# Attention of a hybrid decoder trunk: the value table's two parts side by side, denominators summed on GpSimd, value products two key blocks behind the scores

## The chip, the cores and the metric

One core of one Trainium2 chip runs the whole program. The metric is the device time of one execution in microseconds. All times below are of the kernel before the change.

## The reference

Two decoder layers over 1024 tokens of 1024 features in float32. Layer 0 mixes by attention with a forget gate (8 heads of 64) beside a causal pooling mixer; layer 1 is an RWKV-7 time mix; after each mixer stands a SwiGLU block. The change touches the attention alone:

```python
def one_block(args):
    i, q_i, c_i = args
    q_pos = i * Q_BLOCK + jnp.arange(Q_BLOCK)
    logits = (jnp.einsum('bhqd,bhkd->bhqk', q_i, k).astype(jnp.float32) * scale
              + c_i[..., :, None] - cum[..., None, :])
    causal = key_pos[None, :] <= q_pos[:, None]
    p = jax.nn.softmax(jnp.where(causal, logits, -1e30), axis=-1)
    return jnp.einsum('bhqk,bhkd->bhqd', p.astype(v.dtype), v)
```

## The kernel before, in words

Activations lie with features on the partitions and 512 tokens (one `half`) on the free axis. A product that has to be exact to float32 is split: `part` (L257; its operations are L259 and L260) makes a rounded high part on ScalarE and the rest, the low part, on VectorE. `mm3` (L156) then issues three matmuls per block: high by high (L163), high by low (L164), low by high (L165). Weights are loaded and split the same way in `load_part` (L150 load, L151 ScalarE, L152 VectorE).

The attention, `fox`, works on pairs of heads `p` (0 to 3) and on a head `a` (0, 1) of the pair. For one head:

- `assemble` (L474) copies keys and queries into 128-row tables: high parts in one half of the rows (`own`), low parts in the other (`oth`). The values are transposed into `VH[a][:, :, own]` (high, L492) and `VL[a][:, :, own]` (low, L493). The other 64 columns of `VH` are ones and those of `VL` zeros, set once at the start by GpSimd.
- `maxima` (L496) takes row maxima of the scores; its VectorE reduction is L512. It uses the same PSUM tiles `s` (two) as the scores.
- `attend` (L525) runs 12 steps: for the first half of the queries (`hq` 0) the key blocks `j` 0 to 3, for the second 0 to 7. A step's width `w` is 512 queries, or 384, 256, 128 on the diagonal. `scores` issues two or three matmuls into `s` (L538, L539, mask L541), then ScalarE's exponential `pt` (L543), its rounded part `ph` (a ScalarE cast, L121) and the rest `pl` on VectorE (L547). `values`, one step later, adds three matmuls into the PSUM tile `o`: `VH` by `ph` (L556), `VH` by `pl` (L557), `VL` by `ph` (L558). Because of the ones in `VH`, the other 64 rows of `o` hold the denominator. After the last block of a `hq` the logarithm, a sum with the gate, an exponential and a product (L563 to L566) write the result into `y`.

The order of work is set by `weave`: after each `yield c` of `attend`, the generators beside it are advanced by `c` times their weight. They are the next head's `assemble` and `maxima` (weight 0.5), and a filler of weight 2.8 to 3.2: for `a` = 0 the projections of the next pair (`prep`, with `head`, L425), for `a` = 1 up to three pooling units (`pool_group`, seven in all, L580 to L612, whose parts `pp` are made at L586 and L587 and multiplied at once) and an output gate; for the pair 3 the output projection. A scheduler then places each engine's instructions in one fixed order. Every engine works through its own queue in that order and waits at the head of it.

```python
        for st in steps:
            live.append(scores(*st))
            yield 2 * live[-1][4] / HN + 0.3
            if len(live) > 1:
                yield values(*live.pop(0))
```

GpSimd has few instructions in this part: the pooling unit's small copies and products (L592, L595, L608, L609). The PSUM tile `t` exists once; `head_mean` (L276 to L278), the transposes of `assemble` (L490) and of `maxima` (L518) take turns in it. Scratch tiles `tmp` rotate through five buffers.

Of the kernel before, what the change touches and what calls it, by code (L numbers as in the profile page):

```python
# [9 lines left out]
F32 = mybir.dt.float32  # L10
# [6 lines left out]
P = 128  # L17
# [296 lines left out]
def fox(k, ins, H, hpool, xpools, y, then, r_att):  # L314
# [65 lines left out]
    QB = [ap_.tile([P, S], F32R, tag=f"QB{a}", name=f"QB{a}") for a in range(2)]  # L380
    VH = [ap_.tile([P, 8, P], F32R, tag=f"VH{a}", name=f"VH{a}") for a in range(2)]
    VL = [ap_.tile([P, 8, P], F32R, tag=f"VL{a}", name=f"VL{a}") for a in range(2)]
    for a in range(2):
        own = slice(64 * a, 64 * a + 64)
        oth = slice(64 - 64 * a, 128 - 64 * a)
        nc.gpsimd.memset(QB[a][oth].bitcast(F32), 0.0)
        nc.gpsimd.memset(KB[a][oth].bitcast(F32), 0.0)
        nc.gpsimd.memset(KB[a][64 - 64 * a:72 - 64 * a].bitcast(F32), 1.0)
        nc.gpsimd.memset(VH[a][:, :, oth].bitcast(F32), 1.0)
        nc.gpsimd.memset(VL[a][:, :, oth].bitcast(F32), 0.0)  # L390

# [33 lines left out]
    def head(p, which, half, hl):  # L425

        g = gq if which == "q" else cvec(k, "k_gain")
        o = yield from project(hl, half)
        sq = tmp("asq")[:, 0:HN]
        nc.scalar.activation(sq, o, AF.Square)  # L430
        ms = head_mean(k, sq, [ap_.tile([P, HN], F32R, tag=t, name=nm(k, t), bufs=2) for t in ("ph", "pl")], (onesR, ep[half]))
        yield 3
        ars = tmp("ars")[:, 0:HN]
        nc.scalar.activation(ars, ms, AF.Ln)
        nc.scalar.activation(ars, ars, AF.Exp, scale=-0.5)
        t = ap_.tile([P, HN], F32, tag="a" + which, name=nm(k, "a" + which), bufs=2)
        nc.vector.scalar_tensor_tensor(t, o, g, ars, ALU.mult, ALU.mult)
        getattr(R[p], which)[half] = t
# [35 lines left out]
    def assemble(p, a):  # L474
# [18 lines left out]
        nc.vector.tensor_tensor(VL[a][:, :, own], pvb, rd(VH[a][:, :, own]), ALU.subtract)  # L493
# [31 lines left out]
    def attend(p, a):  # L525

        steps = [(a, hq, j) for hq in range(2) for j in range(4 * hq + 4)]
        live = []
        out = {}

        def scores(a, hq, j):
# [10 lines left out]
            pt = ap_.tile([P, HN], F32, tag="pt", name=nm(k, "pt"), bufs=2)  # L542
            nc.scalar.activation(pt[:, 0:w], s[:, 0:w], AF.Exp, bias=ncumT[:, j, h:h + 1])  # L543
            ph = ap_.tile([P, HN], F32R, tag="ph", name=nm(k, "ph"), bufs=2)
            pl = ap_.tile([P, HN], F32R, tag="pl", name=nm(k, "pl"), bufs=2)
            copy_to(k, CE[2], ph[:, 0:w], pt[:, 0:w])
            nc.vector.tensor_tensor(pl[:, 0:w], pt[:, 0:w], rd(ph[:, 0:w]), ALU.subtract)  # L547
            return a, hq, j, q0, w, ph, pl

        def values(a, hq, j, q0, w, ph, pl):  # L550
# [6 lines left out]
            nc.tensor.matmul(oo, VH[a][:, j], pl[:, 0:w], start=False, stop=False)  # L557
            nc.tensor.matmul(oo, VL[a][:, j], ph[:, 0:w], start=False, stop=(j == nj - 1))  # L558
            if j == nj - 1:
                own = slice(64 * a, 64 * a + 64)  # L560
                oth = slice(64 - 64 * a, 128 - 64 * a)
                den = tmp("den")[:, 0:HN]
                nc.scalar.activation(den[own], o[oth], AF.Ln)  # L563
                nc.vector.tensor_tensor(den[own], den[own], y[p][hq][own], ALU.add)
                nc.scalar.activation(den[own], den[own], AF.Exp, scale=-1.0)
                nc.vector.tensor_tensor(y[p][hq][own], o[own], den[own], ALU.mult)  # L566
            return 3 * w / HN

        for st in steps:
            live.append(scores(*st))  # L570
            yield 2 * live[-1][4] / HN + 0.3
            if len(live) > 1:
                yield values(*live.pop(0))
        for l in live:
            yield values(*l)

# [975 lines left out]
```

## Time and profile before

| what | value |
|---|---|
| time, median of 3 runs | 2701.54 us (2696.48 to 2703.55) |
| the profiled execution | 2699.03 us |
| its span in the trace | 2697.2 us |
| TensorE matmuls busy | 2633.8 us, 98% |
| VectorE busy | 1724.3 us, 64% |
| ScalarE busy | 1301.9 us, 48% |
| GpSimd busy | 50.6 us, 2% |
| attention, from 87 to 467 us: TensorE, VectorE, ScalarE busy | 374.30, 257.93, 213.77 of 380 us |

The profiled execution lies between the lowest and the median run. A matmul's row gives the time from its start to its modelled end; the next matmul starts before that end, so what a matmul takes from the queue is read from the start of one row to the start of the next. PE stands for TensorE's matmuls, PEld for its weight loads, DVE for VectorE, ACT for ScalarE, POOL for GpSimd. A wait row says which engine and line waited, and whose instruction ended the wait.

### The profile page before, as it was taken

The page shows a single profiled execution, that of the slowest core. Times are in us where ns is not written, and L with a number is a line of the kernel's source. Part 1 is how long each engine was busy: PE and PEld are TensorE (multiplying, and loading weights), DVE is VectorE, ACT ScalarE, POOL GpSimd, SP SyncE. Part 2 cuts the span into 40 slices and gives each one's busy share as a digit, 9 for nine tenths or more (in the row PEclk, how much of TensorE's full clock was granted, in tenths as well). Part 3 has the DMA queues.
Part 4 walks back from the last instruction along what each step waited for, and adds up shares of the span by engine and source line. Part 5 has one row for each costly group of instructions (what it writes and reads, how often), then busy time and mean ns, then how long its engine had stood idle before and what let it go on. Part 6 is the DMA issues. An engine that isn't in the chain of part 4 may idle for free.

```text
span 2697.2 us, 40269 instructions
## 1 busy us (share of the span) xinstructions
PE 2633.8 (98%) x15368; PEld 2080.5 (77%) x15368; DVE 1724.3 (64%) x2940; ACT 1301.9 (48%) x2299; POOL 50.6 (2%) x139
## 2 busy tenths in 40 slices
PE   8999999999999999999999999999999999999999
PEld 6787878788888777777777677777777778888887
DVE  8777684654446655975995685469768856634443
ACT  7555564442224765534634466664445444332232
POOL 1000000000001000000000000000000000000000
PEclk9999999999999999999999999999999999999999
DMA  4111131233333546424523534454344336333333
GB/s 136 58 52 55 44 98 48 83 97 96 96 98 114 168 162 191 129 82 123 160 87 100 194 101 161 160 182 128 91 141 134 93 100 199 109 98 94 98 98 94
DMA packets 170817, 307.03 MB, mean 114 GB/s; under 512 B 18928, under 2 KB 25968, under 8 KB 170624
## 3 DMA queue, kind: packets, MB, share of 16 engines
q1 hardware_dynamic: 156800, 279.29, 33.6%
q10 hardware_dynamic: 13824, 25.17, 2.5%
q8 instruction: 120, 1.97, 0.3%
q14 instruction: 73, 0.60, 0.1%
HBM read 257.96 MB, written 46.43 MB: 113 GB/s over the span
## 4 chain that ended last, share of the span: by engine, by line
PE 77%; DVE 14%; DMA 3%; ACT 3%; issue 2%; SPq 0%; DVEq 0%; ACTq 0%
PE mm L163 16%; PE mm L164 16%; PE mm L165 16%; PE fm L163 6%; PE fm L164 5%; PE fm L165 5%; DVE wlo L152 2%; PE mm L175 1%; DVE nu L1108 1%; DVE pd L1106 1%; DMA wraw<-in_wu_dram 1%; DVE ZL L1064 1%; ACT whi L151 1%; PE o L1173 1%; PE s L1161 1%
## 5 line engine op out<-in xcount | busy, mean ns | idle before, releaser
L151 ACT CAST whi<-wraw 128x512 fp32r<-128x512 f32 x738 | 453.7, 617 | 867.4 <-PE mm L164 478.7
L152 DVE TENSOR_TENSOR wlo<-wraw,whi 128x512 fp32r<-128x512 f32 x738 | 501.3, 684 | 449.6 <-ACT whi L151 441.1
L163 PE MATMUL mm<-hh,whi 128*128 128x512 f32 x864 | 344.1, 400 | 6.2 <-ACT hh L355 6.1
L165 PE MATMUL mm<-hh,wlo 128*128 128x512 f32 x864 | 338.4, 392 | 0.0
L164 PE MATMUL mm<-hl,whi 128*128 128x512 f32 x864 | 337.9, 392 | 0.0
L163 PE MATMUL mm<-uh,whi 128*128 128x512 f32 x728 | 283.6, 391 | 0.9 <-DVE x L1317 0.9
L165 PE MATMUL mm<-uh,wlo 128*128 128x512 f32 x728 | 283.1, 390 | 1.0 <-DVE wlo L152 1.0
L164 PE MATMUL mm<-ul,whi 128*128 128x512 f32 x728 | 283.2, 390 | 0.0
L163 PE MATMUL fm<-h1h,whi 128*128 128x512 f32 x528 | 220.2, 417 | 14.8 <-DVE sg L726 9.9
L164 PE MATMUL fm<-h1l,whi 128*128 128x512 f32 x528 | 210.3, 398 | 0.1
L165 PE MATMUL fm<-h1h,wlo 128*128 128x512 f32 x528 | 209.5, 397 | 0.5 <-DVE wlo L152 0.5
L163 PEld LDWEIGHTS mm<-hh,whi 128*128 128x128 f32 x864 | 162.3, 188 | 43.4 <-ACT hh L355 7.8
L165 PEld LDWEIGHTS mm<-hh,wlo 128*128 128x128 f32 x864 | 162.5, 188 | 34.4 <-issue 0.2
L164 PEld LDWEIGHTS mm<-hl,whi 128*128 128x128 f32 x864 | 162.7, 188 | 33.1 <-DVE hl L260 1.7
L163 PE MATMUL fm<-hh,whi 128*128 128x512 f32 x416 | 170.9, 411 | 3.3 <-ACT hh L259 2.3
L164 PE MATMUL fm<-hl,whi 128*128 128x512 f32 x416 | 164.9, 396 | 0.2 <-DVE hl L260 0.2
L165 PE MATMUL fm<-hh,wlo 128*128 128x512 f32 x416 | 164.6, 396 | 0.0
L163 PEld LDWEIGHTS mm<-uh,whi 128*128 128x128 f32 x728 | 136.5, 188 | 34.6 <-issue 3.5
L164 PEld LDWEIGHTS mm<-ul,whi 128*128 128x128 f32 x728 | 136.6, 188 | 30.9 <-issue 1.1
L165 PEld LDWEIGHTS mm<-uh,wlo 128*128 128x128 f32 x728 | 136.7, 188 | 30.1 <-DVE wlo L152 1.8
L705 DVE TENSOR_TENSOR x<-mm,x 128x512 f32<-128x512 f32 x96 | 66.3, 692 | 119.3 <-PE mm L165 119.2
L163 PEld LDWEIGHTS fm<-h1h,whi 128*128 128x128 f32 x528 | 100.6, 191 | 47.1 <-DVE sg L726 12.2
(338 smaller groups left out, 4645.4 us busy)
## 6 DMA issues: line engine op xcount, KB each, us to landing
wraw<-in_wg_dram SPq DMA_DIRECT2D x176, 256.0 KB, 2.8
wraw<-in_wu_dram SPq DMA_DIRECT2D x176, 256.0 KB, 2.7
wraw<-in_wd_dram SPq DMA_DIRECT2D x176, 256.0 KB, 2.7
wraw<-in_w_in_dram SPq DMA_DIRECT2D x52, 256.0 KB, 2.9
x<-in_xT_dram SPq DMA_DIRECT2D x32, 256.0 KB, 4.6
x<-x SPq DMA_DIRECT2D x32, 256.0 KB, 3.3
wraw<-in_w_k_dram SPq DMA_DIRECT2D x32, 256.0 KB, 2.8
wraw<-in_w_v_dram SPq DMA_DIRECT2D x32, 256.0 KB, 3.0
```

Of the source, the lines that this page charges most:

```text
L151: k.nc.scalar.copy(hi[0:p, 0:n], raw[0:p, 0:n])
L152: k.nc.vector.tensor_tensor(lo[0:p, 0:n], raw[0:p, 0:n], rd(hi[0:p, 0:n]), ALU.subtract)
L163: nc.tensor.matmul(out, wh, xh, start=(first and i == 0), stop=False)
L164: nc.tensor.matmul(out, wh, xl, start=False, stop=False)
L165: nc.tensor.matmul(out, wl, xh, start=False, stop=(last and i == n - 1))
L175: k.nc.tensor.matmul(out[n * q:n * q + n], w[:, n * j:n * j + n], xs[j], start=c == 0, stop=c + g == len(xs), tile_position=(0, n * q))
L705: nc.vector.tensor_tensor(X[half][m], o, X[half][m], ALU.add)
L1064: nc.vector.tensor_tensor(ZL[h][HS[1 - h], i, bs], s4[HS[1]], self.msk[HS[1]].rearrange("p a t -> p (a t)").unsqueeze(1).broadcast_to([64, ...
L1106: nc.vector.tensor_tensor(pv, nu[:, j + 1:32, j:j + 1].broadcast_to([P, n, j]), nu[:, j:j + 1, 0:j].broadcast_to([P, n, j]), ALU.mult)
L1108: nc.vector.tensor_tensor(nu[:, j + 1:32, 0:j], nu[:, j + 1:32, 0:j], pv, ALU.add)
L1161: nc.tensor.matmul(z[HS[h], i], ZL[h][:, i, c, 0:64], SV[h][:, i, c], start=True, stop=True)
L1173: nc.tensor.matmul(sp[HS[h], i], BK[h][:, i, c], uv[h][:, i], start=True, stop=True)
```

## The change

1. `VL` goes. The low part of the values is written into the columns of `VH` that held ones, so that one table has the high part in `own` and the low part in `oth`. A step's value products are two matmuls in place of three; `o` then holds high products in its `own` rows and low products in the others.
2. The denominators leave the matmuls. The exponentials of key block 0 go to a tile `da` (two buffers), and GpSimd adds each later block's `pt` to it. At the end of a `hq` the tile is split by `part` and summed over the partitions by two matmuls with `onesR` into `t`.
3. The end of a `hq` becomes a generator, `finish`. Its first half splits `da`, copies the low rows of `o` (ScalarE) and adds them to the high rows (VectorE). Its second half, one step later, holds the two matmuls and the former four operations. For `hq` 1 it runs after the last value product.
4. The value products run two steps behind the scores, and `ph` and `pl` have three buffers in place of two, in `head` too.

`part`, `tmp`, `pst` and `onesR` are those of before.

```diff
...
-        nc.gpsimd.memset(VH[a][:, :, oth].bitcast(F32), 1.0)
-        nc.gpsimd.memset(VL[a][:, :, oth].bitcast(F32), 0.0)
...
-        nc.vector.tensor_tensor(VL[a][:, :, own], pvb, rd(VH[a][:, :, own]), ALU.subtract)
+        nc.vector.tensor_tensor(VH[a][:, :, oth], pvb, rd(VH[a][:, :, own]), ALU.subtract)
...
-            pt = ap_.tile([P, HN], F32, tag="pt", name=nm(k, "pt"), bufs=2)
+            if j == 0:
+                pt = den[a, hq] = ap_.tile([P, HN], F32, tag="da", name=nm(k, "da"), bufs=2)
+            else:
+                pt = ap_.tile([P, HN], F32, tag="pt", name=nm(k, "pt"), bufs=2)
...
-            ph = ap_.tile([P, HN], F32R, tag="ph", name=nm(k, "ph"), bufs=2)
-            pl = ap_.tile([P, HN], F32R, tag="pl", name=nm(k, "pl"), bufs=2)
+            ph = ap_.tile([P, HN], F32R, tag="ph", name=nm(k, "ph"), bufs=3)
+            pl = ap_.tile([P, HN], F32R, tag="pl", name=nm(k, "pl"), bufs=3)
...
+            if j:
+                d = den[a, hq][:, q0 - hq * HN:]
+                nc.gpsimd.tensor_tensor(d, d, pt[:, 0:w], ALU.add)
...
-            nc.tensor.matmul(oo, VH[a][:, j], pl[:, 0:w], start=False, stop=False)
-            nc.tensor.matmul(oo, VL[a][:, j], ph[:, 0:w], start=False, stop=(j == nj - 1))
+            nc.tensor.matmul(oo, VH[a][:, j], pl[:, 0:w], start=False, stop=(j == nj - 1))
             if j == nj - 1:
-                own = slice(64 * a, 64 * a + 64)
-                oth = slice(64 - 64 * a, 128 - 64 * a)
-                den = tmp("den")[:, 0:HN]
-                nc.scalar.activation(den[own], o[oth], AF.Ln)
-                nc.vector.tensor_tensor(den[own], den[own], y[p][hq][own], ALU.add)
-                nc.scalar.activation(den[own], den[own], AF.Exp, scale=-1.0)
-                nc.vector.tensor_tensor(y[p][hq][own], o[own], den[own], ALU.mult)
+                ends.append(finish(a, hq, o, den[a, hq]))
             return 3 * w / HN
+
+        def finish(a, hq, o, d):
...
+            dh, dl = (ap_.tile([P, HN + 16], F32R, tag="tmp", name=nm(k, "dd"), bufs=k.tmpbufs)[:, 0:HN] for _ in range(2))
+            part(k, (dh, dl), d)
+            low = tmp("low")[:, 0:HN]
+            nc.scalar.copy(low[own], o[oth])
+            num = tmp("num")[:, 0:HN]
+            nc.vector.tensor_tensor(num[own], o[own], low[own], ALU.add)
+            yield 2
+            t = pst(k, "t", 1)
+            nc.tensor.matmul(t, onesR, dh, start=True, stop=False)
+            nc.tensor.matmul(t, onesR, dl, start=False, stop=True)
+            nc.scalar.activation(low[own], t[own], AF.Ln, scale=64.0)
+            nc.vector.tensor_tensor(low[own], low[own], y[p][hq][own], ALU.add)
+            nc.scalar.activation(low[own], low[own], AF.Exp, scale=-1.0)
+            nc.vector.tensor_tensor(y[p][hq][own], num[own], low[own], ALU.mult)
+            yield 0
 
         for st in steps:
             live.append(scores(*st))
             yield 2 * live[-1][4] / HN + 0.3
-            if len(live) > 1:
+            if ends and next(ends[0], None) is None:
+                ends.pop()
+            if len(live) > 2:
                 yield values(*live.pop(0))
         for l in live:
             yield values(*l)
+        for e in ends:
+            yield from e
```

Outside the attention the order of every engine is the same as before, but for GpSimd's settings at the start. Three places of the new order are looked at below.

TensorE at the end of head (0, 1), before the change (L538 to L541 scores, L556 to L558 values, L163 to L165 the filler):

```order
L538 MATMUL s_429_1795<-QA1_104,KA1_102 128x128
L539 MATMUL s_429_1795<-QB1_108,KB1_106 128x128
L541 MATMUL s_429_1795<-maskTR_94,identR_93 128x128
L556 MATMUL o_369_1560<-ph_427_1779,VH1_110 128x256
L557 MATMUL o_369_1560<-pl_428_1780,VH1_110 128x256
L558 MATMUL o_369_1560<-ph_427_1779,VL1_112 128x256
L538 MATMUL s_435_1820<-QA0_103,KA0_101 128x512
L539 MATMUL s_435_1820<-QB0_107,KB0_105 128x512
L541 MATMUL s_435_1820<-maskTR_94,identR_93 128x128
L163 MATMUL mm_445_1854<-hh_9_135,whi_439_1842 128x512
L164 MATMUL mm_445_1854<-hl_10_136,whi_439_1842 128x512
L556 MATMUL o_369_1560<-ph_431_1801,VH1_110 128x128
```

and with the change, from the last two value steps of that head on (L561 and L562 values, L579 and L580 the sum of `dd`, the split `da`, into `t`; L536 to L539 scores):

```order
L163 MATMUL mm_436_1776<-hh_100_386,whi_425_1721 128x512
L164 MATMUL mm_436_1776<-hl_101_387,whi_425_1721 128x512
L165 MATMUL mm_436_1776<-hh_100_386,wlo_426_1722 128x512
L561 MATMUL o_397_1623<-ph_439_1789,VH1_110 128x256
L562 MATMUL o_397_1623<-pl_440_1790,VH1_110 128x256
L561 MATMUL o_397_1623<-ph_443_1814,VH1_110 128x128
L562 MATMUL o_397_1623<-pl_444_1815,VH1_110 128x128
L579 MATMUL t_450_1843<-dd_446_1835,onesR_92 128x512
L536 MATMUL s_451_1850<-QA0_103,KA0_101 128x512
L537 MATMUL s_451_1850<-QB0_107,KB0_105 128x512
L539 MATMUL s_451_1850<-maskTR_94,identR_93 128x128
L580 MATMUL t_450_1843<-dd_447_1836,onesR_92 128x512
```

Before, the next head's scores and the filler follow the last values. Now the sum of the denominators stands right behind the last value product, its second half four rows on. Between the head's last mask matmul (six rows ahead of this piece) and L579 stand 12 matmuls.

TensorE in head (0, 0), with the change, where `head_mean` of the filler (L277, L278) and `finish` of `hq` 0 use the tile `t` one after the other:

```order
L165 MATMUL mm_270_1139<-hh_80_341,wlo_222_963 128x512
L163 MATMUL mm_270_1139<-hh_84_350,whi_221_962 128x512
L278 MATMUL t_267_1130<-pl_266_1127,bones_67 128x512
L164 MATMUL mm_270_1139<-hl_85_351,whi_221_962 128x512
L165 MATMUL mm_270_1139<-hh_84_350,wlo_222_963 128x512
L536 MATMUL s_273_1165<-QA0_103,KA0_101 128x512
L537 MATMUL s_273_1165<-QB0_107,KB0_105 128x512
L579 MATMUL t_271_1143<-dd_253_1084,onesR_92 128x512
L580 MATMUL t_271_1143<-dd_254_1085,onesR_92 128x512
```

Between the last matmul into one `t` and the first into the next stand four matmuls; before the change the next use of `t` behind this one came 30 matmuls later.

GpSimd in head (0, 1), with the change (L552 the additions to `da`, the other lines those of the pooling unit):

```order
L552 TENSOR_TENSOR da_315_1345<-da_315_1345,pt_339_1448 128x128
L614 COPY pu_349_1475<-halo_119 128x16
L552 TENSOR_TENSOR da_360_1504<-da_360_1504,pt_366_1535 128x512
L614 COPY pu_382_1584<-halo_119 128x16
L552 TENSOR_TENSOR da_360_1504<-da_360_1504,pt_377_1570 128x512
L617 COPY halo_119<-pu_382_1584 128x16
L630 TENSOR_TENSOR x_385_1592<-pb_384_1589,fc_221 128x16
L631 TENSOR_TENSOR x_385_1592<-x_385_1592,pu_382_1584 128x16
L552 TENSOR_TENSOR da_360_1504<-da_360_1504,pt_400_1642 128x512
```

Before, the rows L614 to L631 stood there alone; now the additions share the queue with them, and one addition stands behind a product that waits for VectorE's pooling sums.

## Rows read from the trace of the kernel before

**Rows 1.** The page: busy time of each engine; shares of the last chain.

```profile
PE 2633.8 (98%) x15368; PEld 2080.5 (77%) x15368; DVE 1724.3 (64%) x2940; ACT 1301.9 (48%) x2299; POOL 50.6 (2%) x139
...
PE 77%; DVE 14%; DMA 3%; ACT 3%; issue 2%; SPq 0%; DVEq 0%; ACTq 0%
```

**Rows 2.** Windows: stretch; busy PE, PEld, DVE, ACT, POOL; clock; DMA share, GB/s.

```profile
87.00:467.00 380.00, 374.30 (x1796) 304.28 (x1795) 257.93 (x531) 213.77 (x393) 7.92 (x24) 1.00 0.18 57
...
250.00:270.00 20.00, 19.36 (x87) 15.02 (x87) 19.56 (x44) 11.02 (x19) 2.08 (x5) 1.00 0.25 85
...
sum 80.00, PE 77.42 PEld 60.37 DVE 75.43 ACT 50.88 POOL 5.02; mean PE 19.35 PEld 15.09 DVE 18.86 ACT 12.72 POOL 1.26
...
sum 80.00, DVE 11.70; mean DVE 2.92
```

**Rows 3.** Timeline of TensorE, 461 to 465 us: start, duration, line, operation.

```profile
461.05 0.33 PE L558 MATMUL o<-ph,VL 128*128 128x384 f32 x1
461.22 0.39 PE L163 MATMUL mm<-hh,whi 128*128 128x512 f32 x1
461.45 0.40 PE L164 MATMUL mm<-hl,whi 128*128 128x512 f32 x1
...
463.88 0.28 PE L558 MATMUL o<-ph,VL 128*128 128x256 f32 x1
464.00 0.39 PE L163 MATMUL mm<-hh,whi 128*128 128x512 f32 x1
...
464.85 0.28 PE L558 MATMUL o<-ph,VL 128*128 128x128 f32 x1
464.97 0.44 PE L163 MATMUL mm<-hh,whi 128*128 128x512 f32 x1
```

**Rows 4.** Waits, 87 to 470 us: who <- for whom: total us, times, longest.

```profile
PEld o L557 <- DVE pl L547: 4.1, 11, 0.6
...
PEld o L556 <- ACT ph L121: 2.3, 4, 0.9
...
PE mm L163 <- ACT pp L586: 1.6, 5, 0.4
...
PE o L557 <- DVE pl L547: 1.2, 5, 0.4
...
PE o L556 <- ACT ph L121: 1.0, 2, 0.5
```

**Rows 5.** Groups by shape, 87 to 470 us: busy, mean ns; idle before, releaser.

```profile
L547 DVE TENSOR_TENSOR pl<-pt,ph 128x512 fp32r<-128x512 f32 x48 | 33.0, 687 | 12.4 <-ACT ph L121 11.9
...
L121 ACT CAST ph<-pt 128x512 fp32r<-128x512 f32 x48 | 29.7, 620 | 2.0 <-PE o L558 0.9
...
L564 DVE TENSOR_TENSOR den<-den,x 64x512 f32<-64x512 f32 x16 | 11.0, 686 | 7.8 <-ACT den L563 7.7
...
L434 ACT ACTIVATE ars<-t 128x512 f32<-128x512 f32 x12 | 7.2, 598 | 14.4 <-PE t L278 14.4
...
L543 ACT ACTIVATE pt<-s,ncumT 128x128 f32<-128x128 f32 x16 | 5.8, 362 | 5.2 <-PE s L541 5.2
```

**Rows 6.** GpSimd's groups by shape, whole span; same columns.

```profile
L389 POOL MEMSET VH<- 128x512 f32 x2 | 1.1, 527 | 0.1
```

**Rows 7.** Timelines of GpSimd and VectorE at 148, 250 and 865 us.

```profile
147.94 0.53 POOL L592 COPY pu<-halo 128x16 f32<-128x16 f32 x1 [27.82 <-DVE x L610]
...
147.73 0.89 DVE L152 TENSOR_TENSOR wlo<-wraw,whi 128x512 fp32r<-128x512 f32 x2
...
250.69 0.22 POOL L609 TENSOR_TENSOR x<-x,pu 128x16 f32<-128x16 f32 x1
...
250.22 0.69 DVE L512 CUSTOM_DVE_ANT_0 s<-s,bc 128x512 f32<-128x512 f32 x1
...
864.99 1.37 POOL L773 COPY x<-hlast 128x1 f32<-128x1 f32 x1
...
865.03 1.29 DVE L152 TENSOR_TENSOR wlo<-wraw,whi 128x512 fp32r<-128x512 f32 x2
```

More of the change, by code (lines that the diff above doesn't have):

```diff
@@ L381, in fox @@
     VH = [ap_.tile([P, 8, P], F32R, tag=f"VH{a}", name=f"VH{a}") for a in range(2)]
-    VL = [ap_.tile([P, 8, P], F32R, tag=f"VL{a}", name=f"VL{a}") for a in range(2)]
     for a in range(2):
@@ L430, in head @@
         nc.scalar.activation(sq, o, AF.Square)
-        ms = head_mean(k, sq, [ap_.tile([P, HN], F32R, tag=t, name=nm(k, t), bufs=2) for t in ("ph", "pl")], (onesR, ep[half]))
+        ms = head_mean(k, sq, [ap_.tile([P, HN], F32R, tag=t, name=nm(k, t), bufs=3) for t in ("ph", "pl")], (onesR, ep[half]))
         yield 3
@@ L527, in attend @@
         steps = [(a, hq, j) for hq in range(2) for j in range(4 * hq + 4)]
-        live = []
-        out = {}
+        live, ends = [], []
+        out, den = {}, {}
         def scores(a, hq, j):
@@ L556, in values @@
             nc.tensor.matmul(oo, VH[a][:, j], ph[:, 0:w], start=(j == 0), stop=False)
-            nc.tensor.matmul(oo, VH[a][:, j], pl[:, 0:w], start=False, stop=False)
-            nc.tensor.matmul(oo, VL[a][:, j], ph[:, 0:w], start=False, stop=(j == nj - 1))
+            nc.tensor.matmul(oo, VH[a][:, j], pl[:, 0:w], start=False, stop=(j == nj - 1))
             if j == nj - 1:
-                own = slice(64 * a, 64 * a + 64)
-                oth = slice(64 - 64 * a, 128 - 64 * a)
-                den = tmp("den")[:, 0:HN]
-                nc.scalar.activation(den[own], o[oth], AF.Ln)
-                nc.vector.tensor_tensor(den[own], den[own], y[p][hq][own], ALU.add)
-                nc.scalar.activation(den[own], den[own], AF.Exp, scale=-1.0)
-                nc.vector.tensor_tensor(y[p][hq][own], o[own], den[own], ALU.mult)
-            return 3 * w / HN
+                ends.append(finish(a, hq, o, den[a, hq]))
+            return 3 * w / HN
+        def finish(a, hq, o, d):
+            own = slice(64 * a, 64 * a + 64)
+            oth = slice(64 - 64 * a, 128 - 64 * a)
+            dh, dl = (ap_.tile([P, HN + 16], F32R, tag="tmp", name=nm(k, "dd"), bufs=k.tmpbufs)[:, 0:HN] for _ in range(2))
[13 more added lines that the diff above has]
+            yield 0
         for st in steps:
```

## The prediction

> **What bounds the kernel now.** Start with the page. TensorE is busy 98% of the span and holds 77% of the chain that ended last [rows 1]; no other engine is near. Outside the attention the order of the work does not change, so only the attention's own stretch is open to this change. There, from 87 to 467 us, TensorE is busy 374.30 of 380 us, VectorE 257.93, ScalarE 213.77, GpSimd 7.92, with the clock granted in full [rows 2]. So the first question is how many matmuls go, and the second is whether the other engines can still feed what is left.
>
> A matmul's duration is misleading for the first question: rows overlap. One 512-column matmul lasts 0.39 us, but the next starts 0.23 us later; 384 columns take 0.17 us from start to start, 256 and 128 take 0.12 us each [rows 3].
>
> For the second question an average hides what matters. Over the whole attention VectorE is busy 68%. In the four stretches 150 to 170, 250 to 270, 350 to 370 and 370 to 390 us, where pooling units, maxima and weight splits meet, it is busy 75.43 of 80 us, and 19.56 of 20 in the second [rows 2]. There TensorE and VectorE are both near their limit. In between VectorE has much idle time.
>
> **The change part by part.**
>
> *A value product less per step.* There are 96 steps (8 heads of 12): 48 of 512 columns and 16 each of 384, 256 and 128. By the start-to-start times [rows 3] the L558 matmuls take 48 x 0.23 + 16 x 0.17 + 32 x 0.12 = 17.6 us. All of it lies on TensorE's queue, which is the path. The work for the low value part in `assemble` stays one VectorE operation per head, written elsewhere; the four memsets that go, 0.53 us each [rows 6], stood at the start on an idle engine and are worth nothing.
>
> *Two matmuls per end.* 16 ends (8 heads, two halves) x 2 x 0.23 = 7.4 us more on TensorE. Net, TensorE's queue is 10.2 us shorter.
>
> *Two steps of distance.* Waits of the value products for `ph` and `pl`: their matmuls stood idle 1.2 + 1.0 = 2.2 us, their weight loads 4.1 + 2.3 = 6.4 us [rows 4]. The first is the least that goes, the second the most, since a weight load's wait is partly covered by the matmul before it. The chain from exponential to `pl` is the exponential, 0.62 and 0.69 us [rows 5], and a step of the weave takes some 4 us (380 us for 96 steps), so one step more covers it. I take 4 us. The third buffers of `ph` and `pl` only allow this.
>
> *The new operations of an end.* ScalarE gets two copies more per end, 32 x 0.62 = 20 us, VectorE two, 32 x 0.69 = 22 us [rows 5]. ScalarE goes from 214 to some 234 of 370 us and stays covered by TensorE's work; if that cover were gone, these would cost their length. VectorE's share matters in the four stretches, below.
>
> *GpSimd's additions.* 80 of them (3 and 7 per head), together 56 widths of 512. The trace of before has no GpSimd addition of this size. The nearest row that writes as much is a memset of 128x512, 527 ns [rows 6]: an addition cannot well be faster. Above, reading twice and writing once in turn would be three such passes, 1.58 us. I take two, 1.05 us, as the two reads are more work than a memset and the write can lie beside them; 56 x 1.05 = 59 us of some 370 is no load for GpSimd by itself. The Trainium skill, "GPSIMD Engine Reference", section "Engine selection", puts two-input operations at about twice VectorE's time; by VectorE's 0.69 us that is an estimate of 1.37 us, inside these bounds, and with it the sum below would gain 4 us less; no run here shows it yet.
>
> What counts is whether an addition holds up VectorE. Small GpSimd operations show that the two interfere: a product of 128x16 takes 0.22 us beside VectorE's L512, which reads PSUM, but a plain copy of 128x16 takes 0.53 us when it meets L152, which reads two SBUF tiles, and a copy of a single column takes 1.37 us under two such operations in a row, ending with the second [rows 7]. The small operations never showed the reverse, a VectorE operation held by GpSimd, because they are too short. Its price per full addition is between nothing and the whole 1.58 us. I take 0.43 us: an addition becomes ready with `pt`, at the same moment as ScalarE's cast, so `pl` comes 0.62 us into its 1.05 us.
>
> In the four stretches L547 fills 11.70 us [rows 2], 17 full widths at 0.69 us; each stretch has an end in it, so some four are first blocks without an addition and 13 remain. VectorE gets there 13 x 0.43 = 5.6 us of holding and 4 x 2 x 0.69 = 5.5 us of new operations. Its idle time there is 80 - 75.43 = 4.6 us. So 6.5 us overflow. The value products have a step to spare, but the pooling unit's second product has none: it waits for `pp` today already [rows 4]. Some of the lag slides into the idle time behind each stretch. I take 5 us lost (0 to 6.5 at this price).
>
> *New waits of TensorE.* (a) In three heads `finish` takes the tile `t` four matmuls, 0.92 us, behind `head_mean`'s last. In between that matmul must end (0.39 us) and ScalarE's logarithm of 0.60 us [rows 5] must read it, so 0.1 us is late at best, 0.7 with one operation ahead of it: 0.3 us x 3. (b) At the end of the three heads with `a` = 1 and a next pair, L579 stands 2.1 us behind the last scores. Scores to the split tile are 0.28 us, an exponential of 0.36, a short addition of about 0.3 and a cast of 0.62 [rows 5], so 1.6 us when all are free, more when GpSimd is held: 0 to 0.7, 0.4 us x 3. (c) Behind the last end the scheduler has put 15 matmuls, 3.5 us, until one needs a PSUM tile that VectorE frees only after the last product of `finish`: 0.39 + 0.60 + 0.69 + 0.63 + 0.69 and the freeing 0.69 make 3.7 us, with hand-overs some 0.8 us late. Together 2.9 us, 0.3 to 5.
>
> *Sum.* -17.6 + 7.4 - 4 + 5 + 2.9 = -6.3 us. On the profiled execution, 2699.03 us, that is 2692.7; it lies 2.5 us under the median of the runs shown, 2701.54, against which the forecast is **2695.2 us**.
>
> **The rivals.**
>
> *VectorE keeps up.* The additions slip between VectorE's operations, or the lag is worked off in the idle time behind each stretch. For it: VectorE idles 122 of 380 us, and two steps of distance were just added. Against: it is at 94 to 98% where the lag arises. Then -10.2 - 4 to -6.4 + 1, so -13 to -16 us: 2685 to 2688.
>
> *The lock decides (slower).* Each addition holds VectorE for all of its length. Place: the four stretches. Price at three passes: 13 x 1.58 + 5.5 - 4.6 = 21.4 us in place of 5, so the sum is +10 us, 2712. It costs more than all gains from 0.8 us held per full addition, and is over 0.3% slower from 1.4 us. For it: GpSimd's waits [rows 7] are as long as VectorE's operations, whole. Against: the next two-input operation after an addition starts is often one cast away. This is the rule of the Trainium skill, "SBUF — State Buffer", section "Who interferes with whom": a VectorE instruction with two SBUF inputs and a GpSimd instruction that reads SBUF exclude each other for a whole instruction. The GpSimd side of it agrees with the 0.53 and 1.37 us; for the VectorE side no run here shows it yet.
>
> *The gain is used up on GpSimd's queue.* One addition stands behind a product that waits for VectorE's pooling sums, and `pt` has two buffers, so a late addition stops the exponential and all behind it on ScalarE. At four such places, one operation of 0.69 us and one addition of 1.05 each, 7 us come on top: about no change, 2702. Against: a step of 4 us passes between two uses of a buffer.
>
> **How the numbers follow.** The forecast's case, a gain of 2 to 10 us, has 0.55, VectorE keeping up 0.25, the lock 0.10, the queue 0.10. Some 0.3%, 8.1 us, is what a measurement of this kernel tells from no change. Faster by more: the second case and a fifth of the first, 0.36. Slower by more: the lock, 0.10. Within: 0.54. The range reaches down to the whole gain without new waits, 2685, less a microsecond for the runs' own spread, and up to half way into the lock's case: 2684 to 2707 us.
>
> **What would show it.** Right: L561 and L562 at 0.23 us from start to start, no L558; 32 new matmuls; few waits of value products; additions near 1 us; `pl` longer than 0.69 us on the mean when it meets one; VectorE without idle time in the four stretches and TensorE's waits there at `pp` and at the scores' tiles. Wrong: additions far above 1.6 us, ScalarE waiting for `pt`, a wait of over a microsecond at each L579, or `pl` unchanged at 0.69 us, which would bring the faster case.

## The result, and the profile after

The median is 2710.89 us (2709.3 to 2714.5), against 2701.64 us for the kernel before in the same rounds: a ratio of 1.0039, 95% interval 1.0026 to 1.0052. The change makes the kernel **slower**, by some 10 us; the forecast of 2695.2 us and its range up to 2707 missed it. The time is that of the rival "the lock decides", 2712 us, though not in the places that it named. The profiled execution's span is 2708.9 us, 11.7 over that of before.

The page of the changed kernel answers to [rows 1]: busy time of each engine, then the shares of the last chain.

```profile
PE 2632.8 (97%) x15304; PEld 2073.6 (77%) x15304; DVE 1766.3 (65%) x2972; ACT 1317.7 (49%) x2331; POOL 134.3 (5%) x215
...
PE 66%; DVE 14%; DMA 3%; ACT 2%; issue 2%; POOL 0%; DVEq 0%; SPq 0%; ACTq 0%; POOLq 0%
```

TensorE has 64 matmuls less, 96 L558 gone and 32 new, as expected, yet is busy almost as long. GpSimd works 84 us more. The shares of the chain add up to some 87%: it goes back no further than 320 us, so it covers only the last part of the attention, and there GpSimd stands in it with a single addition of 0.92 us.

Windows answer to [rows 2], columns as there: the attention, one of the four full stretches, and the sum over all four.

```profile
87.00:467.00 380.00, 363.70 (x1694) 288.13 (x1693) 295.49 (x557) 226.35 (x418) 91.58 (x102) 0.99 0.18 55
...
250.00:270.00 20.00, 19.37 (x87) 15.04 (x87) 19.60 (x42) 12.64 (x22) 6.75 (x8) 1.00 0.23 66
...
sum 80.00, PE 73.54 PEld 56.67 DVE 76.64 ACT 53.81 POOL 25.41; mean PE 18.39 PEld 14.17 DVE 19.16 ACT 13.45 POOL 6.35
```

In the same 380 us TensorE is busy 10.6 us less than before and VectorE 37.6 us more. The four stretches hold only 3.9 us of TensorE's lost time (77.42 to 73.54 of 80), and no more when they are moved along with the work, which lies up to 11 us later here. Most of it is lost elsewhere, where VectorE has idle time on the average.

What TensorE waits for in the attention answers to [rows 4]: who, for whom, total, times, longest.

```profile
PE t L278 <- DVE pl L260: 4.2, 7, 0.9
PE s L507 <- DVE mx L510: 2.9, 2, 1.9
...
PE o L562 <- DVE pl L549: 1.3, 2, 1.0
PE t L516 <- DVE m L514: 1.3, 5, 0.4
PE o L561 <- ACT ph L121: 1.1, 1, 1.1
...
PE t L580 <- DVE dd L260: 1.0, 2, 0.6
...
PEld o L562 <- DVE pl L549: 2.4, 6, 1.1
```

The value products' waits for `pl` did fall on the weight loads, 4.1 to 2.4 us; on the matmuls they did not, 1.2 and 1.3 us. At the top stand waits that [rows 4] did not have: `head_mean` of the filler (L278) for its low part, the row maxima's scores (L507), the transpose L516. All three are released by VectorE and lie away from the value products.

Groups by shape over the attention, as in [rows 5]: busy, mean ns, idle before and its releaser.

```profile
L552 POOL TENSOR_TENSOR da<-da,pt 128x512 f32<-128x512 f32 x32 | 44.5, 1392 | 121.9 <-ACT pt L545 121.9
...
L549 DVE TENSOR_TENSOR pl<-pt,ph 128x512 fp32r<-128x512 f32 x32 | 30.4, 949 | 4.6 <-ACT ph L121 4.2
...
L549 DVE TENSOR_TENSOR pl<-pt,ph 128x256 fp32r<-128x256 f32 x16 | 9.7, 608 | 10.2 <-ACT ph L121 10.1
...
L545 ACT ACTIVATE pt<-s,ncumT 128x512 f32<-128x512 f32 x32 | 22.0, 687 | 19.6 <-PE s L537 16.8 <-DVE mx L510 2.4 <-PE s L539 0.2
```

A 128x512 addition lasts 1.39 us on the mean. `pl`, 687 ns before, is 949 ns now; the `pl` of each first block, which has no addition, stayed at 685. The exponential never waits for GpSimd.

The timelines of GpSimd and VectorE around 165 and 201 us show what happens at one addition, and answer to [rows 7] (start, duration, engine, line):

```profile
165.49 1.80 POOL L552 TENSOR_TENSOR da<-da,pt 128x512 f32<-128x512 f32 x1 [3.55 <-ACT pt L545]
...
201.22 1.29 POOL L552 TENSOR_TENSOR da<-da,pt 128x512 f32<-128x512 f32 x1 [8.03 <-ACT pt L545]
```

```profile
165.44 0.69 DVE L584 TENSOR_TENSOR x<-num,low 64x512 f32<-64x512 f32 x1
166.16 0.70 DVE L510 CUSTOM_DVE_ANT_0 s<-s,bc 128x512 f32<-128x512 f32 x1
...
166.88 0.95 DVE L549 TENSOR_TENSOR pl<-pt,ph 128x512 fp32r<-128x512 f32 x1
...
201.82 1.23 DVE L549 TENSOR_TENSOR pl<-pt,ph 128x512 fp32r<-128x512 f32 x1 [0.45 <-ACT ph L121]
```

The addition of 201.22 ends at 202.51; `pl`, begun at 201.82, ends at 203.05, 0.54 us behind it. The one of 165.49 met L584 first, which reads two SBUF tiles, and was itself held, to 1.80 us. It ended at 167.29, and `pl` ended 0.54 us later, at 167.83. In between L510, which reads PSUM, ran through in 0.70 us. This is the exclusion that the Trainium skill, "SBUF — State Buffer", section "Who interferes with whom", describes; now both sides of it are seen.

### The profile page after: what moved, and what is told of

Its sections match the earlier page's. It is cut to its first block, busy times and chain, and to the rows that moved or that the text cites. A ratio compares the mean times of both kernels' runs of the same rounds, so it can differ in the third digit from the quotient of the medians.

```text
span 2708.9 us, 40345 instructions
## 1 busy us (share of the span) xinstructions
PE 2632.8 (97%) x15304; PEld 2073.6 (77%) x15304; DVE 1766.3 (65%) x2972; ACT 1317.7 (49%) x2331; POOL 134.3 (5%) x215
## 4 chain that ended last, share of the span: by engine, by line
PE 66%; DVE 14%; DMA 3%; ACT 2%; issue 2%; POOL 0%; DVEq 0%; SPq 0%; ACTq 0%; POOLq 0%
PE mm L163 14%; PE mm L164 14%; PE mm L165 14%; PE fm L163 6%; PE fm L164 5%; PE fm L165 5%; DVE wlo L152 2%; DMA wraw<-in_wu_dram 1%; DVE nu L1130 1%; DVE pd L1128 1%; DVE ZL L1086 1%; PE mm L175 1%; PE o L1195 1%; PE s L1183 1%; PE s L1189 1%
## 5 line engine op out<-in xcount | busy, mean ns | idle before, releaser
L152 DVE TENSOR_TENSOR wlo<-wraw,whi 128x512 fp32r<-128x512 f32 x738 | 502.0, 684 | 436.7 <-ACT whi L151 432.7
L163 PE MATMUL mm<-hh,whi 128*128 128x512 f32 x864 | 345.9, 401 | 9.2 <-ACT hh L355 5.9
L165 PE MATMUL mm<-hh,wlo 128*128 128x512 f32 x864 | 339.2, 393 | 0.0
L163 PE MATMUL mm<-uh,whi 128*128 128x512 f32 x728 | 283.5, 391 | 0.9 <-DVE x L1339 0.9
L165 PE MATMUL mm<-uh,wlo 128*128 128x512 f32 x728 | 283.0, 389 | 0.4 <-DVE wlo L152 0.4
L163 PE MATMUL fm<-h1h,whi 128*128 128x512 f32 x528 | 220.2, 417 | 15.0 <-DVE sg L748 10.0
L165 PE MATMUL fm<-h1h,wlo 128*128 128x512 f32 x528 | 209.8, 398 | 0.0
L163 PEld LDWEIGHTS mm<-hh,whi 128*128 128x128 f32 x864 | 162.9, 189 | 46.7 <-ACT hh L355 6.6
L165 PEld LDWEIGHTS mm<-hh,wlo 128*128 128x128 f32 x864 | 163.2, 189 | 34.7 <-issue 0.2
L163 PE MATMUL fm<-hh,whi 128*128 128x512 f32 x416 | 172.0, 414 | 3.2 <-ACT hh L259 2.5
L165 PE MATMUL fm<-hh,wlo 128*128 128x512 f32 x416 | 165.6, 398 | 0.0
L163 PEld LDWEIGHTS mm<-uh,whi 128*128 128x128 f32 x728 | 136.5, 188 | 34.5 <-issue 3.5
L165 PEld LDWEIGHTS mm<-uh,wlo 128*128 128x128 f32 x728 | 136.7, 188 | 29.0 <-DVE wlo L152 0.8
L163 PEld LDWEIGHTS fm<-h1h,whi 128*128 128x128 f32 x528 | 100.8, 191 | 47.2 <-DVE sg L748 12.5
```

Source lines behind the costliest of these rows:

```text
L152: k.nc.vector.tensor_tensor(lo[0:p, 0:n], raw[0:p, 0:n], rd(hi[0:p, 0:n]), ALU.subtract)
L163: nc.tensor.matmul(out, wh, xh, start=(first and i == 0), stop=False)
L165: nc.tensor.matmul(out, wl, xh, start=False, stop=(last and i == n - 1))
```

## The experiments

Beside totals I use the **attention stretch**: from the first score matmul to the first matmul behind the attention that reads `uh`. It is cleaner than the total, in which the unchanged part (span less stretch) varies from 2289.5 to 2298.3 us between the profiled executions. How much the stretch varies between executions of one kernel was not measured, so little hangs on its last microsecond. Its two ends in the tile views of before (duration min/median/max, first and last start):

```profile
L538 PE MATMUL s<-QA,KA x96: 220/389/499, 85.2 to 462.6; 128*128 128x512 f32 x48, 128*128 128x384 f32 x16, 128*128 128x256 f32 x16, 128*128 128x128 f32 x16
...
L163 PE MATMUL mm<-uh,whi x728: 388/389/793, 492.9 to 1040.0; 128*128 128x512 f32 x182
```

and of the changed kernel:

```profile
L536 PE MATMUL s<-QA,KA x96: 220/389/688, 84.8 to 469.7; 128*128 128x512 f32 x48, 128*128 128x384 f32 x16, 128*128 128x256 f32 x16, 128*128 128x128 f32 x16
...
L163 PE MATMUL mm<-uh,whi x728: 388/389/793, 502.7 to 1048.7; 128*128 128x512 f32 x182
```

Before: 492.9 - 85.2 = 407.7 us. After: 502.7 - 84.8 = 417.9 us. So 10.2 of the 11.7 us between these two executions lie in the attention. All stretches below are worked out in this way, each from the one profiled execution. My theory was that the additions hold VectorE; the rivals were the new ends, the second step, and the number of TensorE's instructions.

| run | ratio to before, 95% interval | stretch |
|---|---|---|
| changed kernel | 1.0039 (1.0026 to 1.0052) | 417.9 |
| without additions | 0.9997 (0.9984 to 1.0010) | 403.1 |
| before, with additions | 1.0038 (1.0026 to 1.0051) | 417.8 |
| changed, one step | 1.0046 (1.0029 to 1.0063) | 415.9 |
| before, two steps | 1.0005 (0.9996 to 1.0015) | 409.6 |
| additions on VectorE | 1.0007 (0.9998 to 1.0017) | 406.9 |
| additions in parts | 1.0036 (1.0023 to 1.0049) | 414.5 |
| memsets instead | 0.9988 (0.9976 to 0.9999) | 403.0 |
| no additions, one step | 1.0012 (1.0003 to 1.0022) | 405.3 |
| VectorE, more casts on ScalarE | 1.0004 (0.9992 to 1.0015) | 406.2 |
| additions behind `pl` | 1.0059 (1.0045 to 1.0072) | 424.3 |
| VectorE, one step | 1.0027 (1.0017 to 1.0036) | 413.0 |
| before, two products | 0.9947 (0.9933 to 0.9961) | 391.8 |

**Without the additions.** The denominators are then those of the first key block alone, plus one.

```diff
-            if j:
-                d = den[a, hq][:, q0 - hq * HN:]
-                nc.gpsimd.tensor_tensor(d, d, pt[:, 0:w], ALU.add)
...
-            nc.scalar.activation(low[own], t[own], AF.Ln, scale=64.0)
+            nc.scalar.activation(low[own], t[own], AF.Ln, scale=64.0, bias=1.0)
```

> The changed kernel without GpSimd's additions (L552): the denominators are those of the first key block alone, with a one added before the logarithm; all else stays. Theory H: the additions hold VectorE for their whole length (its operations in the attention grew by 20 us in all), and that lateness is what TensorE waits for. Then the 128x512 subtraction of pl is back at 0.69 us and the time falls by 8 to 14 us, to 2697 to 2703 us. Rival R: the waits come from the end's new operations, from the tile t and from the new order; then the time stays within 3 us of 2711 us, with pl shorter all the same.

The stretch falls by 14.8 us to 403.1, 4.6 below before. `pl` is back at its old length:

```profile
L549 DVE TENSOR_TENSOR pl<-pt,ph 128x512 fp32r<-128x512 f32 x32 | 22.0, 688 | 5.1 <-ACT ph L121 4.9
```

So the 80 additions turn a change that is worth nothing on the whole (ratio 0.9997) into a loss. Not all of the 14.8 us need be the hold: without the additions the scheduler also places some 30 of VectorE's operations elsewhere, the splits of `da` above all, and some 25 matmuls. The next run keeps the order.

**The additions alone, on the kernel before.** They go into a tile that nothing reads; the constant columns of the two value tables are shared to make room. The orders of TensorE, VectorE and ScalarE are those of before.

```diff
...
+            if j == 0:
+                den[a, hq] = ap_.tile([P, HN], F32, tag="da", name=nm(k, "da"), bufs=1)
+                nc.gpsimd.memset(den[a, hq], 0.0)
+            else:
+                d = den[a, hq][:, q0 - hq * HN:]
+                nc.gpsimd.tensor_tensor(d, d, pt[:, 0:w], ALU.add)
```

> The kernel before, with GpSimd's 80 additions of pt into a tile that nobody reads (the two heads' value tables share their 64 constant columns to make room; the order of TensorE, VectorE and ScalarE is that of before, row for row). Theory H: the additions alone hold VectorE as in the change, pl (128x512) goes from 0.69 to 0.9 us or more, and the time rises by 8 to 14 us, to 2709 to 2715 us. Rival R: additions are harmless without the end's new operations and the new order: within 3 us of 2701 us.

The stretch grows by 10.1 us, the total by 0.38%, with the same instructions in the same order on the other engines and nobody waiting for the sum. `pl` again:

```profile
L549 DVE TENSOR_TENSOR pl<-pt,ph 128x512 fp32r<-128x512 f32 x48 | 44.1, 918 | 11.8 <-ACT ph L121 11.2
```

The hold by itself is therefore enough for the loss.

**One step of distance, with the additions.**

```diff
-            if len(live) > 2:
+            if len(live) > 1:
```

> The changed kernel with the value products one step behind the scores again (three buffers kept). If the second step hides the late pl as predicted: 3 to 8 us slower than the change, 2714 to 2719 us, with longer waits of L561 and L562. If the second step only moved waits to other places: within 2 us of 2711 us. If the new order is itself the cause of the waits at L278, L507 and L516: faster by 3 us or more.

Stretch 415.9, ratio 1.0046 (2714.4 us, at the lower edge of the range expected for a useful second step): not told apart from the changed kernel's 1.0039. The second step neither makes the loss nor buys much.

**Two steps, on the kernel before.**

```diff
...
-            ph = ap_.tile([P, HN], F32R, tag="ph", name=nm(k, "ph"), bufs=2)
-            pl = ap_.tile([P, HN], F32R, tag="pl", name=nm(k, "pl"), bufs=2)
+            ph = ap_.tile([P, HN], F32R, tag="ph", name=nm(k, "ph"), bufs=3)
+            pl = ap_.tile([P, HN], F32R, tag="pl", name=nm(k, "pl"), bufs=3)
...
-            if len(live) > 1:
+            if len(live) > 2:
```

> The kernel before with the value products two steps behind and three buffers of ph and pl, nothing else (value tables sharing their constant columns for room). By the prediction's term the waits of the value products go: 3 to 7 us faster than before, 2694 to 2698 us. If the second step only moves waits to other instructions: within 2 us of 2701 us.

Stretch 409.6, 1.9 more than before, ratio 1.0005. The step alone gains nothing here.

**The additions on VectorE.**

```diff
-                nc.gpsimd.tensor_tensor(d, d, pt[:, 0:w], ALU.add)
+                nc.vector.tensor_tensor(d, d, pt[:, 0:w], ALU.add)
```

> The changed kernel with the additions on VectorE. Theory H: VectorE then has 80 operations more, 56 full widths at 0.60 us from start to start, 34 us, in place of some 20 us of being held: 4 to 12 us slower than the change, 2715 to 2723 us. Rival R, by which VectorE's load does not set the time: within 3 us of 2711 us. Faster than 2707 us would say that the hold costs more than its length.

```profile
L552 DVE TENSOR_TENSOR da<-da,pt 128x512 f32<-128x512 f32 x32 | 22.0, 688 | 3.8 <-ACT pt L545 3.6
```

VectorE gets some 34 us more to do, and the stretch is 406.9: 3.8 more than without additions, where GpSimd cost 14.8. The time, 2702.9 us, misses both ranges above and falls into the third case, that the hold costs more than its length. Giving the work to the idle engine was dearer than giving it to the one with the load.

**In parts of 128 columns.** If whole instructions exclude each other, short ones should hold for less.

```diff
-                d = den[a, hq][:, q0 - hq * HN:]
-                nc.gpsimd.tensor_tensor(d, d, pt[:, 0:w], ALU.add)
+                for c in range(0, w, P):
+                    d = den[a, hq][:, q0 - hq * HN + c:q0 - hq * HN + c + P]
+                    nc.gpsimd.tensor_tensor(d, d, pt[:, c:c + P], ALU.add)
```

> The changed kernel with each addition cut into pieces of 128 columns, 224 in place of 80. A piece of 128 took 0.46 us alone, a whole of 512 1.30 us. Theory H with a lock for one instruction: VectorE gets in after 0.46 us at most, the mean of pl (128x512) falls from 0.95 us to 0.75 to 0.85 us and the time by 2 to 6 us, to 2705 to 2709 us. If GpSimd's next piece takes the lock again before VectorE: pl as long or longer (1.85 us for four pieces), and the time equal or up to 5 us more. Rival R: no change in time whatever pl does.

```profile
L549 DVE TENSOR_TENSOR pl<-pt,ph 128x512 fp32r<-128x512 f32 x32 | 26.5, 828 | 5.0 <-ACT ph L121 4.6
...
L553 POOL TENSOR_TENSOR da<-da,pt 128x128 f32<-128x128 f32 x224 | 134.1, 626 | 228.2 <-ACT pt L545 211.1 <-DVE pl L549 17.0
```

`pl` comes down from 949 to 828 ns and the stretch to 414.5. The sign is right, though the ratio, 1.0036, does not tell the time from the changed kernel's. GpSimd then works 134 us, and 11.4 of the 14.8 us remain; some 1.7 of them are the price of one half-clock period (last section).

**GpSimd busy, without reading.** Two memsets of the tile (it is set to a constant) in place of each addition; as in the first run, the later key blocks are missing from the denominators.

```diff
-                nc.gpsimd.tensor_tensor(d, d, pt[:, 0:w], ALU.add)
+                nc.gpsimd.memset(d[:, 0:w], 0.0)
+                nc.gpsimd.memset(d[:, 0:w], 0.0)
...
```

> The changed kernel with each addition replaced by two GpSimd memsets of the same columns of da, which write SBUF and read nothing, some 1.06 us for 512 columns (the denominators are left out, with a one added before the logarithm). If VectorE is held only while GpSimd reads SBUF: pl at 0.69 us and the time as without additions, 2697 to 2701 us. If any GpSimd instruction on SBUF holds it: pl at 0.85 us or more and 2706 to 2711 us.

```profile
L549 DVE TENSOR_TENSOR pl<-pt,ph 128x512 fp32r<-128x512 f32 x32 | 22.0, 688 | 4.6 <-ACT ph L121 4.3
...
L552 POOL MEMSET da<- 128x512 f32 x32 | 16.8, 526 | 52.7 <-DVE pl L549 51.4
```

Stretch 403.0, as without additions, with GpSimd busy for 70 us of it (93 with the additions). The 34 VectorE operations of 512 columns with two SBUF inputs that began under such a memset lasted 680 to 694 ns. The queue and the tiles' dependences cost nothing; it is the reading addition that holds VectorE.

**No additions, one step.** The first edit and the third together.

> The changed kernel without additions (as the first run of this study) and with the value products one step behind. If the second step is worth nothing, as the run on the kernel before says, where the waits only moved: within 2 us of the run without additions, 2697 to 2701 us. If it covers what the new operations of the end make late: 2702 to 2706 us.

Stretch 405.3; the time, 2703.5 us, is that of the second case. With the run without additions this gives the second step's worth where nothing holds VectorE, 2.2 us; with the one-step run, the additions' worth at one step, 415.9 - 405.3 = 10.6 us.

**Additions on VectorE, casts off it.** The copies of `QA` and `KB` go to ScalarE as well.

```diff
-    CE="VVA"
+    CE="AAA"
...
```

> The variant with the additions on VectorE, and the two copies of keys and queries in assemble (0.42 us each, 24 between 87 and 470 us, more in all) moved from VectorE to ScalarE. If VectorE's load sets the waits that are left: 2 to 5 us faster than that variant's 2702.9 us, 2698 to 2701 us. If ScalarE is then late instead, or the waits have another cause: within 2 us, or slower.

Stretch 406.2, with one half-clock period in it, ratio 1.0004: not told apart from the run with the additions on VectorE. VectorE's load is at most a small part of what is left.

**Additions only behind `pl`.** I thought that the hold hurts because it falls on `pl`, which the value products want. Here each addition waits for the `pl` of its own block.

```diff
-            nc.vector.tensor_tensor(pl[:, 0:w], pt[:, 0:w], rd(ph[:, 0:w]), ALU.subtract)
+            low = nc.vector.tensor_tensor(pl[:, 0:w], pt[:, 0:w], rd(ph[:, 0:w]), ALU.subtract)
...
-                nc.gpsimd.tensor_tensor(d, d, pt[:, 0:w], ALU.add)
+                i = nc.gpsimd.tensor_tensor(d, d, pt[:, 0:w], ALU.add)
+                tc.add_manual_dep(i.ins, low.ins.name, ...)
```

> The changed kernel with each addition made to wait for the same block's pl, so that it cannot hold that operation. If the cost comes from the hold falling on pl, which is always one cast behind the addition's start: pl (128x512) close to 0.69 us, VectorE's operations stretched by 12 us or less in all, and the time falls by 4 to 8 us, to 2703 to 2707 us. If the hold only moves to VectorE's next operation with two SBUF inputs: stretched by 18 us or more, and the time within 2 us of 2711 us.

```profile
L549 DVE TENSOR_TENSOR pl<-pt,ph 128x512 fp32r<-128x512 f32 x32 | 22.0, 688 | 4.7 <-ACT ph L121 4.4
...
L152 DVE TENSOR_TENSOR wlo<-wraw,whi 128x512 fp32r<-128x512 f32 x50 | 38.2, 764 | 9.3 <-ACT whi L151 9.1
```

and L152 in the changed kernel, same columns:

```profile
L152 DVE TENSOR_TENSOR wlo<-wraw,whi 128x512 fp32r<-128x512 f32 x52 | 36.6, 703 | 9.4 <-ACT whi L151 9.2
```

This theory fell, and neither of the expected cases came whole. `pl` is at 688 ns, but the stretch is 424.3, the longest of all. It has 13.65 us at half the granted clock against the changed kernel's 6.82, which is some 3.4 of the 6.4 us between them. The hold moved to other operations with two SBUF inputs: the weight split L152 is 764 ns here, 703 in the changed kernel. But there is not more of it: all VectorE operations together lasted 18.5 us longer than unheld, against 23.7 in the changed kernel (worked out in the next section). What also changed is that the additions come later, and ScalarE's split of `da` waits for them (who, for whom, total, times, longest):

```profile
ACT dd L259 <- POOL da L552: 11.3, 9, 1.9
```

In the changed kernel these waits are 2.2 us in six places. The run does not separate the two: that the hold falls on worse places, and that the ends come later.

**Additions on VectorE, one step.** The edits of the fifth and the third run.

> The variant with the additions on VectorE and the value products one step behind: with what these runs say so far the best complete version of the new layout. If the second step is worth nothing: within 2 us of that variant, 2701 to 2705 us, no better than before. If it made waits of its own there too: 2697 to 2700 us.

Stretch 413.0, ratio 1.0027; the time, 2707.1 us, lies above both expected ranges. Two periods of 3.41 us at half the granted clock lie in it, which cost some 3.4 us. So about 2.7 of the 6.1 us against two steps are left for the step itself.

**The kernel before without L558.** What the removed product cost, alone; the low part of the values is left out.

```diff
-            nc.tensor.matmul(oo, VH[a][:, j], pl[:, 0:w], start=False, stop=False)
-            nc.tensor.matmul(oo, VL[a][:, j], ph[:, 0:w], start=False, stop=(j == nj - 1))
+            nc.tensor.matmul(oo, VH[a][:, j], pl[:, 0:w], start=False, stop=(j == nj - 1))
```

> The kernel before without the L558 matmuls and nothing else: the low part of the values is left out. By the prediction's term their 17.6 us all lie on TensorE's queue: 14 to 18 us faster, 2683 to 2687 us. If VectorE sets the pace in the four busy stretches and takes part of it back: 7 to 12 us faster, 2689 to 2694 us.

```profile
L163 PE MATMUL mm<-uh,whi x728: 388/389/793, 476.9 to 1023.7; 128*128 128x512 f32 x182
```

Stretch 476.9 - 85.1 = 391.8: 15.9 us less than before.

## Why the prediction was wrong

The runs form a chain from the kernel before to the changed one, one part at a time. The forecast's 5 us for the full stretches served two parts: without any holding, 5.5 - 4.6 = 0.9 us of it would have stayed, for the operations of the ends, so 4.1 us were for the additions.

| part | forecast | stretch | from |
|---|---|---|---|
| L558 goes | -17.6 | -15.9 | before, two products - before |
| ends: two matmuls, new operations, order and waits | 7.4 + 2.9 + 0.9 = +11.2 | +13.5 | no additions, one step - the last |
| second step | -4 | -2.2 | without additions - the last |
| additions on GpSimd | +4.1 | +14.8 | changed - the last |
| sum | -6.3 | +10.2 | |

By the ratios instead of the stretches, at 2701 us, the four parts are -14, +18, -4 and +11 us, each uncertain by some 4 to 5: the same picture, with the ends dearer.

- **The step that failed** is "In the four stretches ... 13 remain", in *GpSimd's additions*. The price was close: 0.43 us held per full addition was forecast. Summing what every VectorE operation of the attention lasted beyond the median of its form in the kernel before gives 23.7 us, over 56 full widths 0.42 us each; in the kernels without additions that sum is at most 1.1. That the price fits is in part luck: it was meant for `pl`, but a `pl` of 512 columns lost 0.26 us on the mean (949 to 687 ns), and 10 of the 23.7 us fell on other operations. What failed is the count and what I set it against: I charged 13 of the 56, those in the full stretches, and set them against VectorE's idle time. "VectorE has much idle time" elsewhere is true of the average. Yet at any one moment TensorE's next matmul wants one certain result, and a result that comes 0.5 us later is late in a stretch that is 68% full as well. The row of L278 above says so: `pl` of `head_mean` cost 4.2 us in seven waits, during the heads with `a` = 0, outside the stretches that I had named. The three longest of these waits came about in the same way, here the first of them. An addition held `assemble`'s L480; the two `pl` behind it in VectorE's queue ran at their own length, but late:

```profile
108.88 1.67 DVE L480 TENSOR_TENSOR KA<-ak,KA 64x512 fp32r<-64x512 f32 x1
110.59 0.69 DVE L549 TENSOR_TENSOR pl<-pt,ph 128x512 fp32r<-128x512 f32 x1
111.20 0.68 DVE L260 TENSOR_TENSOR pl<-asq,ph 128x512 fp32r<-128x512 f32 x1
...
111.93 0.49 PE L278 MATMUL t<-pl,bones 128*128 128x512 f32 x1 [0.90 <-DVE pl L260]
```

  Without the additions L480 takes its own length and L278 does not wait:

```profile
109.02 0.69 DVE L480 TENSOR_TENSOR KA<-ak,KA 64x512 fp32r<-64x512 f32 x1
...
111.08 0.50 PE L278 MATMUL t<-pl,bones 128*128 128x512 f32 x1
```

- The loss of 14.8 us adds up. TensorE's waits on matmuls, all rows of the waits view over the attention summed, are 7.4 us without additions and 17.7 with them: 10.3 us more. Two half-clock periods (last section) add some 3.4. The rest, 1.1 us, is within the growth of the weight loads' waits, 32.3 to 44.3 us. On the kernel before and with one step, where no such period occurred, the additions cost 10.1 and 10.6 us; the first of these, with the order kept, is the price of the hold alone, on that kernel.
- **The ends** were under-priced by 2 us in the stretch, by more in the ratios. Against the kernel with two products, matmul waits rose by 3.3 us (6.6 to 9.9) and weight loads' by 8.4 (24.2 to 32.6), beside the new matmuls' own time. What of it is VectorE's new work, what the tile `t` and what the new order was not separated.
- **The second step** was over-priced by the stretches (2.2 us gained without additions); by the ratios it is as forecast, within their uncertainty. The 2.2 us of matmul waits that I called the least that goes did not go in the changed kernel: its value products wait 1.1 us for `ph` and 1.3 for `pl`. With the additions or on the kernel before, nothing measurable was gained; with the additions on VectorE, about 2.7.
- **L558** at start-to-start times was right within 1.7 us; the matmul count was right. The 7.4 us of the new matmuls were not measured by themselves.
- The rival **"the lock decides"** had the mechanism and by chance the sum, but put 1.58 us on 13 additions where 0.42 us on 56 is what happened. **"VectorE keeps up"** is refuted by `pl`'s 949 ns together with the 10.1 us of unread additions: the lag was not worked off in time. **"The gain is used up on GpSimd's queue"** is refuted by the exponential's row, with no wait for GpSimd, and by the run with memsets.
- For the addition itself I took 1.05 us. It is 1.29 us alone, 1.39 on the mean. The estimate by the Trainium skill, "GPSIMD Engine Reference", section "Engine selection", about twice VectorE's time, was nearer: 1.29 to 0.69 is 1.9.

Why 34 us of additions on VectorE cost 3.8 us and the hold of 23.7 us cost 14.8 is not shown. One reading is that the scheduler places an operation of VectorE's own behind urgent ones, while a hold falls on whatever runs. No complete version of the new layout beat the kernel before: the two best, with the additions on VectorE, stand at 1.0004 and 1.0007, both intervals with 1 inside.

## What to carry to other kernels

An idle GpSimd is no free adder while VectorE runs operations with two SBUF inputs (or casts, last section): here each full addition took 0.42 us from VectorE at moments that nobody chose, and cost the attention 14.8 us where the same additions on VectorE cost 3.8. Price such a hold over every place where it falls, and set it against the slack of the result that is late, never against the idle time of the held engine. A run with the suspect work added to the old kernel, its result unread and the other engines' order kept, gives the price of the hold by itself.

## What the runs showed of the hardware

**The hold has a fixed tail.** A VectorE operation of 512 columns with two SBUF inputs that begins under an addition ends 0.55 us after the addition's end, wherever it began; 0.41 us for 384 columns, 0.28 for 256, 0.15 for 128. That is each time some 0.14 us less than its own length (0.69, 0.55, 0.43, 0.29); one that began in the addition's last 0.14 us kept its length. Operations with an input in PSUM run through, as L510 above, and memsets by GpSimd held no operation with two SBUF inputs.

**Casts are held too.** VectorE's copies of `QA` and `KB` (a cast, 64x512, one SBUF input) take at most 0.43 us in every run without GpSimd additions. The one that began under an addition in the changed kernel took 0.57 us, and with the additions behind `pl` three took 0.67 to 1.12 us. They ended some 0.28 us after the addition's end. No cast began under a memset, so that pair stays open.

**The clock fell inside the attention.** Before, the granted clock there was 1.00 throughout. In the changed kernel two stretches of 3.41 us stood at 0.50, which is the level of 1.2 GHz (columns as in [rows 2]):

```profile
286.92:290.33 3.41, 3.41 (x9) 2.64 (x10) 2.96 (x5) 2.80 (x5) 0.00 (x0) 0.50 0.23 77
...
375.67:379.08 3.41, 3.41 (x12) 2.74 (x11) 3.39 (x7) 2.00 (x4) 2.02 (x2) 0.50 0.39 126
```

TensorE's timeline at the two places:

```profile
284.02 0.33 PE L561 MATMUL o<-ph,VH 128*128 128x128 f32 x1 [1.14 <-ACT ph L121]
284.74 0.33 PE L562 MATMUL o<-pl,VH 128*128 128x128 f32 x1 [0.38 <-DVE pl L549]
...
286.78 0.69 PE L580 MATMUL t<-dd,onesR 128*128 128x512 f32 x1 [0.61 <-DVE dd L260]
...
287.69 0.63 PE L165 MATMUL mm<-hh,wlo 128*128 128x512 f32 x1
288.12 0.63 PE L163 MATMUL mm<-hh,whi 128*128 128x512 f32 x1
...
374.12 0.50 PE L507 MATMUL s<-KA,QA 128*128 128x512 f32 x1 [1.86 <-DVE mx L510]
374.46 0.39 PE L562 MATMUL o<-pl,VH 128*128 128x512 f32 x1
374.69 0.39 PE L163 MATMUL mm<-hh,whi 128*128 128x512 f32 x1
```

Ahead of the first drop TensorE had waited 1.14, 0.38 and 0.61 us within 4 us; ahead of the second, 1.86 us at once. At 0.50 a 512-column matmul follows the last after 0.43 us (287.69 to 288.12) instead of 0.23 (374.46 to 374.69, as in [rows 3]), so each of the two costs some 1.7 us. That the waits brought the drops on is read from their order in time, and no run tested it; if so, a wait can cost more than its own length. The run with the additions behind `pl` had three such drops, two of 3.41 us and one of 6.83.
